# TensorE in the program's own order in one loop, with doubled buffers for attention weights and a longer distance between scores and transposes

## The chip, the cores and the metric

The kernel runs on one core of a Trainium2 chip. Five engines work side by side, each on its own instruction queue: TensorE (PE, matrix products and transposes), VectorE (DVE), ScalarE (ACT), GpSimd (POOL) and SyncE (SP, which here issues all DMA transfers). They tell each other of finished work by semaphores. The metric is the device time of one execution in microseconds (us), median of several.

## The reference

One inference step of a hybrid encoder layer: 2048 prompt frames and 32 sample frames of width 1024, all in 32-bit floats. The input is normalised and modulated, then projected to queries (8 heads of 64), keys and values (2 heads) and an input for a state-space model. One half of the layer is attention in a sliding window, the other half the state-space model with a gate. Both are normalised, joined, and sent through one output projection:

```python
merged = jnp.concatenate([_rmsnorm(attn, lw['attn_out_g']), _rmsnorm(ssm_o, lw['ssm_out_g'])], axis=-1)
x = x + g1 * (merged @ lw['w_out'])
```

with, for the attention,

```python
m = jnp.maximum(jnp.max(s, axis=-1), sink)
p = jnp.exp(s - m[..., None])
p = p / (jnp.sum(p, axis=-1) + jnp.exp(sink - m))[..., None]
o = jnp.einsum('bngrqk,bnkgd->bnqgrd', p, v.astype(jnp.float32))
```

and for the gate `g * sigmoid(g @ ssm_glu_w + ssm_glu_b)` with `g = gelu(ssm_y)`. A feed-forward part (SwiGLU, width 2816) follows and makes up more than half of the time.

## The kernel before

**Precision.** Every product is made of three: each operand is split into a high part that TensorE takes at its fast 32-bit rate (type fp32r) and a low rest, and high x high, high x low and low x high are added up (`mm3`). A split costs one copy, mostly on ScalarE, and one subtraction on VectorE or GpSimd. This is why nearly everything that TensorE makes has to pass through ScalarE and VectorE before TensorE can use it again.

**Stages.** First the input projections with the tables of the state-space model; then the state-space model, 32 groups, with the first six attention tiles beside it; then the loop that the change is about; then the feed-forward part.

**Tiles and flows.** Tokens are worked on in 17 tiles of 128 (the last one is the 32 sample frames), in the order `TILES`: frames 1024 to 2047 first. Each kind of work is written as a Python generator that emits a few instructions and then yields. A `Flow` (L890) holds the generators of one kind that are open: `Flow(make, n, width, lag)` lets at most `width` be open, starts the next one when the youngest has made `lag` steps, and each call of `step` advances every open one by one step, the oldest first.

**One attention tile** (`attention_tile`, L1097). Step 1 loads its rows of queries, keys and values. Step 2 splits and transposes them: the query transposes qb (eight) and the key transposes kb (four). Steps 3 and 4 make the scores s of one half of the queries each (o = 0 and 1), eight matmuls, and call `softmax`: row maxima on VectorE (tile st), exponentials on ScalarE into `pe_[o]` (the trace calls it pbuf), sums and their reciprocal on VectorE, and one multiplication on GpSimd. The next steps, one for each half and each of the two key heads, transpose the weights back through TensorE (`p_split`, L1063: four transposes pt, then the split into th and tl), and after both heads of a half `p_values` multiplies with the values (twelve matmuls ob) and two copies bring the result to the tile att. There are two pbuf buffers, one for each half, and every tile uses the same two. Columns that a half never writes are set to zero once, ahead of all tiles.

**The loop** (the `while True` at L1613) advances four flows in each round, in this order: `fa`, the attention tiles that are still to come; `fp`, the gate of the state-space output (`c_prep`, nine units of 256 frames, so one unit for two tiles; four steps of twelve matmuls cb each, then tanh, products and splits into mh and ml, and a sum of squares ss); `fq`, `c_norm` (sums of squares sa of att, its split into ah and al, and the tiny matmuls rb that turn sums into the factors rso of the two norms); and, in two steps, `fc`, `c_out` (the output projection: two halves of 24 matmuls co for att and 24 for the gate's output, each followed by ScalarE, VectorE and GpSimd and a store). A tile of `c_out` takes five rounds: four with two groups of six co each, and one without. A new attention tile may start only when a tile of `c_out` has ended (six att buffers), so one starts every five rounds. When all attention tiles are done, `h_steps` loads the finished rows xf again and transposes them (ft) for the feed-forward part, at two steps a round.

**Memory of TensorE's results.** Attention takes its result banks in turn from a pair (tag ab) and from the four banks of tag cb, which gate and norms use too; co has two of its own.

**What sets the order.** The generators only set the order in which instructions are emitted. The compiler's planner then makes a plan in time for all engines with its own costs, and each engine's queue is written in the order of that plan, so an instruction emitted later can stand ahead of an earlier one that the plan finds not ready. On the chip each queue then runs strictly in that written order: if an instruction waits, all behind it wait.

Of the kernel before, what the change touches and what calls it, by code (L numbers as in the profile page):

```python
# [10 lines left out]
F32 = mybir.dt.float32  # L11
# [12 lines left out]
NT = NPT + 1  # L24
# [18 lines left out]
NATT = 6  # L43
ASTART = 0
CWS = 2
# [3 lines left out]
CST = 2  # L49
# [8 lines left out]
FA2, CG, WN = 1, 1, 8  # L58
# [15 lines left out]
def hybrid_kernel(  # L74
# [10 lines left out]
    V, A, P, PE, SP = nc.vector, nc.scalar, nc.gpsimd, nc.tensor, nc.sync  # L85
# [17 lines left out]
    def f(a):  # L103
        return a.bitcast(F32)
# [103 lines left out]
    def advance(g, n=1):  # L208
        for _ in range(n):
            if next(g, None) is None:  # L210
                return
# [704 lines left out]
    pb_ = bin_.enter_context(tc.tile_pool(name="pb", bufs=1, reuse_waits="tile", side="right"))  # L916
# [106 lines left out]
    ts(V, nsink, nsink, -1.0)  # L1023
    ts(V, nsinks, nsinks, -1.0)

    pe_ = [pb_.tile([128, 4, 256], F32, name=f"pbuf{o}") for o in range(2)]
    P.memset(pe_[0][:, :, 192:256], 0.0)
    P.memset(pe_[1][:, :, 0:64], 0.0)

    def kv_split(kf, vf, dst, n):  # L1030

# [31 lines left out]
    def p_split(pbuf, kbs, npair, kv):  # L1063

        nc_ = npair * 128
        pt = bbank([128, 2, 256], nm="pt")
        for i in range(npair):
            for kb in kbs:
                PE.transpose(pt[:, kb, i * 128:(i + 1) * 128], pbuf[:, kv * npair + i, kb * 128:kb * 128 + 128], ident)
        th = pb2.tile([128, 2, 256], F32R, tag="th", name="th")  # L1070
        tl = pb2.tile([128, 2, 256], F32R, tag="tl", name="tl")
        k0, k1 = kbs[0], kbs[-1] + 1
        split(th[:, k0:k1, 0:nc_], tl[:, k0:k1, 0:nc_], pt[:, k0:k1, 0:nc_], A, V)
        return th, tl
# [20 lines left out]
    atts = {}  # L1095

    def attention_tile(j):  # L1097
        j = TILES[j]
        n = 128 if j < NPT else DEC
        qkv = pb2.tile([128, QKV], F32, tag="qkv", name="qkv", bufs=1)  # L1100
        SP.dma_start(qkv[0:n], qkv_d[j * 128:j * 128 + n])
        yield 1
        qs = pb2.tile([128, NH, 128], F32R, tag="qs", name="qs", bufs=1)
        qv = qkv[0:n, 0:512].rearrange("p (h d) -> p h d", d=HD)
        split(qs[0:n, :, 0:64], qs[0:n, :, 64:128], qv, A, P)
        qt = pb2.tile([128, NH * 128], F32R, tag="qt", name="qt", bufs=1)
        qw = n // 2 if j < NPT else n
        qtv = qt[:, 0:NH * n].rearrange("p (o h q) -> p h o q", h=NH, q=qw)
        for hb in range(2):
            qb = bbank([128, 4, 128], F32R, nm="qb")  # L1110
            for i in range(4):
                PE.transpose(qb[:, i, 0:n], qs[0:n, hb * 4 + i], identr[0:n, 0:n])
            cp(V if hb else A, qtv[:, hb * 4:hb * 4 + 4], f(qb[:, :, 0:n]).rearrange("p h (o q) -> p h o q", q=qw))
        kf = qkv[0:n, 512:640].rearrange("p (h d) -> p h d", d=HD)
        vf = qkv[0:n, 640:768].rearrange("p (h d) -> p h d", d=HD)
        kt = pb2.tile([128, 4, 256], F32R, tag="kt", name="kt")
        att = pat.tile([128, 4, 128], F32, tag="att", name="att", bufs=NATT)
        atts[j] = att
        if j < NPT:
            vcur = kv_split(kf, vf, kt[:, :, 128:256], n)  # L1120
            if j == TILES[0]:
                pkv = pb2.tile([128, 2, 128], F32, tag="ckv", name="pkv", bufs=1)
                SP.dma_start(pkv, qkv_d[(j - 1) * 128:j * 128, 512:768].rearrange("t (a d) -> t a d", a=2))
                vprev[0] = kv_split(pkv[:, 0].rearrange("p (h d) -> p h d", d=HD),
                                    pkv[:, 1].rearrange("p (h d) -> p h d", d=HD), kt[:, :, 0:128], 128)
            elif j:
                V.tensor_copy(kt[:, :, 0:128], f(vprev[1][:, :, 128:256]))
            vpt = [vprev[0], vcur]
            vprev[0], vprev[1] = vcur, kt
            yield 1  # L1130
            vlist = [(vpt[0], 128), (vcur, 128)]
            kbs = (0, 1) if j else (1,)
            for o in range(2):
                lo, hi = (64 * o, 192 + 64 * o) if j else (128, 192 + 64 * o)
                sp = [bbank([128, 2, 256], nm="s") for _ in range(2)]
                for pr in range(4):
                    for x in range(2):
                        mm(sp[pr // 2][:, pr % 2, lo:hi], qt[:, 512 * o + 128 * pr:512 * o + 128 * pr + 128],
                           kt[:, (pr // 2) * 2 + x, lo:hi], x == 0, x == 1)
                softmax(sp, pe_[o], lo, hi, nsink)  # L1140
                yield 1
            for o in range(2):
                parts = []
                for kv in range(2):
                    parts.append(p_split(pe_[o], kbs, 2, kv))
                    yield 1
                p_values(parts, vlist, kbs, 2, att[:, :, 64 * o:64 * o + 64])
        else:
            ckv = pb2.tile([128, 2, 128], F32, tag="ckv", name="ckv", bufs=1)
            SP.dma_start(ckv[:, 0], cache_k[0, 0].rearrange("t h d -> t (h d)"))  # L1150
            SP.dma_start(ckv[:, 1], cache_v[0, 0].rearrange("t h d -> t (h d)"))
            vc = kv_split(ckv[:, 0].rearrange("p (h d) -> p h d", d=HD), ckv[:, 1].rearrange("p (h d) -> p h d", d=HD),
                          kt[:, :, 0:128], 128)
            vo = kv_split(kf, vf, kt[:, :, 128:160], n)
            sp = bbank([128, 2, 256], nm="s")
            for kv in range(2):
                for x in range(2):
                    mm(sp[:, kv, 0:160], qt[:, 128 * kv:128 * kv + 128], kt[:, kv * 2 + x, 0:160], x == 0, x == 1)
            P.memset(pe_[0][:, 0:2, 160:192], 0.0)
            softmax([sp], pe_[0], 0, 160, nsinks)  # L1160
            yield 1
            parts = [p_split(pe_[0], (0, 1), 1, kv) for kv in range(2)]
            yield 1
            p_values(parts, [(vc, 128), (vo, DEC)], (0, 1), 1, att[:, :, 0:DEC])
        yield 1
# [23 lines left out]
    def stage(nm):  # L1189
        return pw1.tile([128, 512], F32, tag="tc", name=nm, bufs=TC)  # L1190

    fa = Flow(attention_tile, NT, 2, 5)
    n = 0
    while fd.next < fd.n or fd.live:
        for fl, st, lim in ((fm, FM, G), (fd, FDS, G), (fa, FAS, NATT)):
# [21 lines left out]
    cg = chain(glu_steps(wide), wo_steps(range(4), wide, D))  # L1217
# [17 lines left out]
    fp = mbank([128, 64], nm="fp")  # L1235
# [174 lines left out]
    fp_ = {}  # L1410

    def left_open():

        pcg_.close()
        fp_["v"] = ctx.enter_context(tc.tile_pool(name="pfv", bufs=1, reuse_waits="tile", side="right"))

    def ffn_open():

        bin_.close()
        fp_["q"] = ctx.enter_context(tc.tile_pool(name="pfq", bufs=1, reuse_waits="tile", side="right"))  # L1420
        fp_["t"] = ctx.enter_context(tc.tile_pool(name="fst", bufs=2, space=bass.MemoryType.PSUM, reuse_waits="tile"))
# [61 lines left out]
    layers = [Layer(sb, i) for sb in range(3) for i in range(4)]  # L1483
    steps = [(L, u, p) for L in layers for u in range(L.units) for p in range(7)]
    raw, left, right = {}, {}, {}
# [12 lines left out]
    def start_unit(n):  # L1498

        if n < len(steps) and steps[n][0].i == 0:  # L1500
            L, u, _ = steps[n]
            raw[L, u] = [{t: quarter(L, u, m, t, wtile(4)) for t in ("21", "22", "11", "12")} for m in range(2)]
            for r in raw[L, u]:
                r["s1"] = wtile(4)
                tt(P, r["s1"], r["21"], r["22"], ADD)
                tt(P, r["21"], r["11"], r["21"], SUB)
                r["s3"] = r["21"]
# [99 lines left out]
    cg = wo_steps(range(4, 8), stage, 512)  # L1607
    fp = Flow(c_prep, 9, 1, 0)
    fq = Flow(c_norm, NT, 1, 0)
    fc = Flow(c_out, NT, 1, 0)  # L1610
    wn = 0
    hg = [None]
    while True:  # L1613
        more = fa.step(fc.done() + NATT)
        fp.step(fc.done() // 2 + 2)
        for _ in range(CWS):
            wn += 1
            advance(cg)
        fq.step(min(fa.done(), 2 * fp.done(), fc.done() + 2))
        if wn > WN:  # L1620
            for _ in range(CST):
                more = fc.step(fq.done()) or more
        if fa.next == fa.n and not fa.live:
            if hg[0] is None:
                ffn_open()
                hg[0] = h_steps(0)
            elif fc.done() >= 6:
                if (layers[0], 0) not in raw:
                    start_unit(0)
                advance(hg[0], 2)  # L1630
                if fp.next == fp.n and not fp.live and "v" not in fp_:
                    left_open()
                    prepare(0)
        if not more:
            break
    if hg[0] is None:
        ffn_open()
        hg[0] = h_steps(0)
# [199 lines left out]
```

## Time and profile before

| | us |
|---|---|
| median of 3 runs | 2383.77 (2382.73 to 2385.17) |
| profiled execution | 2380.64, its span 2378.8 |
| TensorE busy | 2221.1 (93%) |
| VectorE busy | 1802.9 (76%) |
| ScalarE busy | 1259.6 (53%) |
| GpSimd busy | 1349.8 (57%) |
| first co | 572.45 |
| last att of the loop | 894 |
| first matmul of the feed-forward part | 963 |

Busy shares are averages over stages with different limits; a matmul's time in the trace also contains its way through the array, so the distance from start to start tells more of the rate than a matmul's own duration. The trace's columns in the lists by time are: start, length, engine, line, operation, what is written and read, shapes, count, and in brackets the idle time of the engine before it and what ended it.

### The profile page before, as it was taken

Reading aid. Unit: us, or ns where it says so; the run is one execution under the profiler, and the core shown is the slowest. Engines: PE = TensorE matmul, PEld = TensorE weight load, DVE = VectorE, ACT = ScalarE, POOL = GpSimd, SP = SyncE. Lnnn points to the kernel's source line nnn. Section 1 sums busy time; section 2 is a strip of 40 time slices with the busy share of each in tenths; the row PEclk is TensorE's granted clock in tenths of the full one; section 3 lists DMA queues with packets and bytes.
Section 4 is the critical chain, followed back from the end, with each engine's and each line's share of the span. In section 5 each row is a group of like instructions: output and inputs, shape, how many; then the busy total and the mean of one; then the engine's idle time right before and its main releaser. Section 6 shows DMA issues by size and latency. Waiting matters only on the chain. (4 is left out here: it accounts for less than half of the span.)

```text
span 2378.8 us, 39058 instructions
## 1 busy us (share of the span) xinstructions
PE 2221.1 (93%) x13262; PEld 2058.2 (87%) x13262; DVE 1802.9 (76%) x2722; ACT 1259.6 (53%) x2549; POOL 1349.8 (57%) x1205
## 2 busy tenths in 40 slices
PE   7898998997999999699999998999999989999998
PEld 4577777786888878598999998999999979999998
DVE  6878876777777765877768879666688896777887
ACT  5655534556556556433445556444455754444663
POOL 1277765785655656899654236655532375665232
PEclk8898998999899999799999999999999999999999
DMA  7757767875312214698335644543355435434653
GB/s 229 264 169 232 205 202 220 250 229 157 91 56 76 78 49 153 198 277 252 116 108 159 195 141 151 172 139 101 112 184 174 132 122 175 134 95 121 193 158 123
DMA packets 429572, 380.12 MB, mean 160 GB/s; under 512 B 57326, under 2 KB 358986, under 8 KB 429372
## 3 DMA queue, kind: packets, MB, share of 16 engines
q1 hardware_dynamic: 429372, 377.63, 51.9%
q8 instruction: 104, 1.70, 0.3%
q14 instruction: 96, 0.79, 0.1%
HBM read 284.63 MB, written 92.91 MB: 159 GB/s over the span
## 5 line engine op out<-in xcount | busy, mean ns | idle before, releaser
L89 DVE TENSOR_TENSOR wl<-wr,wh 128x512 fp32r<-128x512 f32 (+1 forms) x714 | 736.0, 1048 | 220.4 <-ACT wh L101 217.5
L101 ACT ACTIVATE wh<-wr 128x512 fp32r<-128x512 f32 (+1 forms) x714 | 434.6, 616 | 540.6 <-PE fx L117 303.2
L117 PE MATMUL fx<-bh,wh 128*128 128x352 f32 (+1 forms) x1584 | 511.6, 323 | 9.7 <-ACT c L101 5.8
L117 PE MATMUL fx<-bl,wh 128*128 128x352 f32 (+1 forms) x1584 | 509.5, 322 | 3.5 <-DVE bl L89 3.5
L117 PE MATMUL fx<-bh,wl 128*128 128x352 f32 (+1 forms) x1584 | 510.3, 322 | 0.0
L89 POOL TENSOR_TENSOR wr<-wr 128x512 f32<-128x512 f32 x264 | 392.6, 1495 | 165.7 <-DVE wl L89 148.0
L117 PEld LDWEIGHTS fx<-bh,wh 128*128 128x128 f32 x1584 | 300.3, 190 | 11.7 <-ACT c L101 6.5
L117 PEld LDWEIGHTS fx<-bl,wh 128*128 128x128 f32 x1584 | 300.0, 189 | 4.1 <-DVE bl L89 4.0
L117 PEld LDWEIGHTS fx<-bh,wl 128*128 128x128 f32 x1584 | 299.5, 189 | 0.1
L117 PE MATMUL fy<-bh,wh 128*128 128x352 f32 (+1 forms) x792 | 255.6, 323 | 2.9 <-DVE acc L98 2.6
L117 PE MATMUL fy<-bh,wl 128*128 128x352 f32 (+1 forms) x792 | 255.0, 322 | 0.1
L117 PE MATMUL fy<-bl,wh 128*128 128x352 f32 (+1 forms) x792 | 254.8, 322 | 0.0
L89 POOL TENSOR_TENSOR c<-c 128x352 f32<-128x352 f32 (+1 forms) x99 | 146.7, 1482 | 173.1 <-ACT wh L101 107.9
L89 POOL TENSOR_TENSOR c<-c,acc 128x352 f32<-128x352 f32 (+1 forms) x72 | 84.5, 1178 | 173.3 <-ACT c L101 169.8
L89 POOL TENSOR_TENSOR q<-q,q 128x1408 f32<-128x1408 f32 (+3 forms) x24 | 86.2, 3596 | 122.9 <-DVE q L89 86.8
L117 PEld LDWEIGHTS fy<-bh,wh 128*128 128x128 f32 x792 | 150.2, 190 | 3.4 <-DVE acc L98 2.9
L89 DVE TENSOR_TENSOR bl<-q,bh 128x1408 fp32r<-128x1408 f32 (+3 forms) x84 | 149.4, 1780 | 5.0 <-ACT bh L101 5.0
L117 PEld LDWEIGHTS fy<-bl,wh 128*128 128x128 f32 x792 | 150.0, 189 | 0.0
L117 PEld LDWEIGHTS fy<-bh,wl 128*128 128x128 f32 x792 | 149.5, 189 | 0.5 <-DVE wl L89 0.4
L117 PE MATMUL fz<-bh,wl 128*128 128x352 f32 (+1 forms) x396 | 130.5, 330 | 10.9 <-DVE wl L89 10.7
L117 PE MATMUL fz<-bh,wh 128*128 128x352 f32 (+1 forms) x396 | 129.5, 328 | 6.5 <-ACT wh L101 6.5
L101 ACT ACTIVATE bh<-q 128x1408 fp32r<-128x1408 f32 (+3 forms) x84 | 107.6, 1284 | 50.3 <-DVE q L89 29.1
(384 smaller groups left out, 5236.3 us busy)
## 6 DMA issues: line engine op xcount, KB each, us to landing
wr<-in_w_gate_dram SPq DMA_DIRECT2D x132, 256.0 KB
wr<-in_w_up_dram SPq DMA_DIRECT2D x132, 256.0 KB
wr<-sd_d SPq DMA_DIRECT2D x96, 256.0 KB
wr<-in_w_down_dram SPq DMA_DIRECT2D x72, 256.0 KB
adw<-in_w_ada_dram SPq DMA_DIRECT2D x64, 256.0 KB
f_d<-c SPq DMA_DIRECT2D x88, 176.0 KB
sm<-sm_d SPq DMA_DIRECT2D x32, 448.0 KB
q<-f_d SPq DMA_DIRECT2D x16, 704.0 KB
```

The costliest lines, as they stand in the source:

```text
L89: e.tensor_tensor(out, a, b, op=op)
L101: A.activation(out, a, func, **kw)
L117: PE.matmul(out, lhsT, rhs, start=start, stop=stop, skip_group_check=more)
```

## The change

It has three parts. The pair of pbuf buffers exists twice, and even and odd tiles take turns. The attention flow may hold three open tiles instead of two, and a tile has two more steps that emit nothing: one between its scores and the first transposes of its weights, one between the last such transposes and the last product with the values. And the whole loop stands in a region in which TensorE's instructions keep the order in which the program emits them; the order of the other engines, and how TensorE's instructions from outside the region fall among them, stay the planner's.

```diff
-    pe_ = [pb_.tile([128, 4, 256], F32, name=f"pbuf{o}") for o in range(2)]
-    P.memset(pe_[0][:, :, 192:256], 0.0)
-    P.memset(pe_[1][:, :, 0:64], 0.0)
+    pes = [[pb_.tile([128, 4, 256], F32, name=f"pbuf{i}{o}") for o in range(2)] for i in range(2)]
+    for pe_ in pes:
+        P.memset(pe_[0][:, :, 192:256], 0.0)
+        P.memset(pe_[1][:, :, 0:64], 0.0)
...
     def attention_tile(j):
+        pe_ = pes[j % 2]
         j = TILES[j]
...
                 softmax(sp, pe_[o], lo, hi, nsink)
                 yield 1
+            yield 1
             for o in range(2):
                 parts = []
                 for kv in range(2):
                     parts.append(p_split(pe_[o], kbs, 2, kv))
+                    yield 1
+                if o:
                     yield 1
                 p_values(parts, vlist, kbs, 2, att[:, :, 64 * o:64 * o + 64])
...
-    fa = Flow(attention_tile, NT, 2, 5)
+    fa = Flow(attention_tile, NT, 3, 5)
...
-    while True:
-        more = fa.step(fc.done() + NATT)
...
+    with tc.manual_schedule(engines={PE.engine}):
+        while True:
+            more = fa.step(fc.done() + NATT)
...
```

The body of the loop is the same but for its indent.

More of the change, by code (lines that the diff above doesn't have):

```diff
@@ L1612, in hybrid_kernel @@
     hg = [None]
-    while True:
-        more = fa.step(fc.done() + NATT)
[L1615 to L1635, printed above, removed]
+    with tc.manual_schedule(engines={PE.engine}):
+        while True:
+            more = fa.step(fc.done() + NATT)
+            fp.step(fc.done() // 2 + 2)
+            for _ in range(CWS):
+                wn += 1
+                advance(cg)
+            fq.step(min(fa.done(), 2 * fp.done(), fc.done() + 2))
+            if wn > WN:
+                for _ in range(CST):
+                    more = fc.step(fq.done()) or more
+            if fa.next == fa.n and not fa.live:
+                if hg[0] is None:
+                    ffn_open()
+                    hg[0] = h_steps(0)
+                elif fc.done() >= 6:
+                    if (layers[0], 0) not in raw:
+                        start_unit(0)
+                    advance(hg[0], 2)
+                    if fp.next == fp.n and not fp.live and "v" not in fp_:
+                        left_open()
+                        prepare(0)
+            if not more:
+                break
     if hg[0] is None:
```

## The prediction

> **What bounds the kernel now.** I read the page first, then the busy time by stretches, then TensorE's waits in the one stretch that the change touches, then the instructions around those waits in order of time.
>
> ```profile
> span 2378.8 us, 39058 instructions
> 640.00:890.00 250.00, 229.35 (x1432) 203.78 (x1432) 182.49 (x312) 136.76 (x397) 148.39 (x133) 0.95 0.20 64
> 888.10:963.00 74.90, 70.80 (x390) 57.87 (x391) 38.82 (x56) 42.75 (x83) 51.65 (x47) 0.96 0.48 158
> ```
>
> The loop of attention, gate and output projection runs from about 565 to 963 us. In its steady part (640 to 890) the columns after the length are the busy times of TensorE, its weight loads, VectorE, ScalarE and GpSimd, then the granted clock. TensorE is busy 229 of 250 us, VectorE only 182: TensorE sets the length, so what can be won there is its idle time, 20.7 us, and what the clock of 0.95 costs, 250 x 0.05 = 12.5 us. The tail (888 to 963) is as tight, and the feed-forward part follows it. I take that part to move as a block with the loop's end.
>
> ```profile
> PE pt L1069 <- POOL pbuf L89: 10.8, 4, 5.3
> PE pt L1069 <- DVE st L89: 3.7, 1, 3.7
> PE co L117 <- DVE t L98: 2.2, 2, 1.1
> PE ob L117 <- DVE tl L89: 2.0, 1, 2.0
> ```
>
> These are TensorE's waits of 640 to 890: 18.7 us, and 14.5 of it before pt, the transposes of the attention weights, which wait for the normalised weights pbuf. Two such places, with the last gate matmul (cb) ahead of each:
>
> ```profile
> 675.33 0.28 PE L117 MATMUL cb<-gh,gll 128*128 128x256 f32 x1
> ...
> 682.02 0.97 PE L117 MATMUL s<-kt,qt 128*128 128x64 f32 x8
> ...
> 686.91 0.39 PE L117 MATMUL ob<-tl,vs 128*128 128x256 f32 x1 [2.04 <-DVE tl L89]
> ...
> 688.88 0.63 PE L117 MATMUL co<-woh,ml 128*128 128x512 f32 x1
> ...
> 693.18 0.69 PE L1069 MATMUL pt<-cpk,pbuf 128*128 128x128 f32 x2 [3.67 <-DVE st L89]
> ...
> 720.04 0.28 PE L117 MATMUL cb<-gl,glh 128*128 128x256 f32 x1
> ...
> 721.22 0.28 PE L117 MATMUL cb<-gh,gll 128*128 128x256 f32 x1
> ...
> 722.52 0.46 PE L1112 MATMUL qb<-identr,qs 128*128 128x128 f32 x4
> ...
> 723.53 0.47 PE L117 MATMUL co<-wol,ah 128*128 128x512 f32 x1
> ...
> 727.50 1.03 PE L117 MATMUL s<-kt,qt 128*128 128x192 f32 x8
> ...
> 730.92 0.42 PE L117 MATMUL co<-woh,ah 128*128 128x512 f32 x1
> ...
> 736.19 0.39 PE L117 MATMUL co<-woh,ml 128*128 128x512 f32 x1
> 741.85 1.12 PE L1069 MATMUL pt<-cpk,pbuf 128*128 128x128 f32 x4 [5.27 <-POOL pbuf L89]
> ```
>
> I number attention tiles from 0 in the order worked on; these are 8 and 10. From the first score matmul (s) to the first pt it takes 693.18 - 682.02 = 11.2 us and 741.85 - 727.50 = 14.35 us. It is the even tiles that stall, because a gate unit serves two tiles and its end throws a burst of splits at VectorE, ahead of the row maxima that the softmax needs:
>
> ```profile
> 735.23 1.64 DVE L89 TENSOR_TENSOR gl<-gr,gh 128x512 fp32r<-128x512 f32 x1
> ...
> 737.36 0.16 DVE L89 TENSOR_TENSOR st<-st,nsink 128x4 f32<-128x4 f32 x1
> ```
>
> The minimum that starts tile 10's softmax (st) comes ten us after its scores. Tiles 12 and 14 do the same, odd tile 9 does not:
>
> ```profile
> 703.08 1.03 PE L117 MATMUL s<-kt,qt 128*128 128x192 f32 x8
> ...
> 775.77 1.48 PE L117 MATMUL s<-kt,qt 128*128 128x192 f32 x12
> ...
> 790.49 0.77 PE L1069 MATMUL pt<-cpk,pbuf 128*128 128x128 f32 x5 [0.18 <-POOL pbuf L89]
> ...
> 826.64 1.03 PE L117 MATMUL s<-kt,qt 128*128 128x192 f32 x8
> ...
> 840.37 0.90 PE L1069 MATMUL pt<-cpk,pbuf 128*128 128x128 f32 x3 [4.87 <-POOL pbuf L89]
> ```
> ```profile
> 710.17 1.47 POOL L89 TENSOR_TENSOR pbuf<-pbuf,st 128x768 f32<-128x768 f32 x1
> ```
>
> That is 14.7 and 13.7 us for 12 and 14, and 710.17 + 1.47 - 703.08 = 8.55 us for 9.
>
> **The change part by part.** *Doubled buffers and a third live tile.* Two more memsets on GpSimd:
>
> ```profile
> L1027 POOL MEMSET pbuf<- 128x256 f32 x1 | 0.3, 317 | 5.6 <-PE adv L117 5.6
> ```
>
> Two at 0.32 us, behind 5.6 us of idle time: nothing, 0.6 us without that cover. A buffer alone also wins nothing here, since exp does not wait for pt to free pbuf:
>
> ```profile
> L101 ACT ACTIVATE pbuf<-s,st 128x192 f32<-128x192 f32 (+3 forms) x77 | 30.7, 412 | 33.8 <-DVE st L89 31.7 <-PE cb L117 2.1
> ```
>
> 31.7 of the 33.8 us are VectorE's minima. The buffers only make the longer distance legal. Tiles still start every five rounds of the loop, so each round's work stays the same. No DMA and no arithmetic is added, and the queues of SP and the other engines stay the planner's.
>
> *TensorE in program order, distance one round longer.* I laid out the rounds from the code, with prices from the rows: co (736.19 - 730.92)/23 = 0.229 us, so the 12 of a round 2.75; cb (721.22 - 720.04)/10 = 0.118, so 12 of them, or the 12 ob of equal width, 1.42; four each of qb, kb and pt take 723.53 - 722.52 = 1.01, so a qb/kb set of 12 is 1.0 and a pt group 0.34; eight s at most 1.0. For an even tile the order between the last cb and its s is: co, pt, qb/kb, co, ob, pt = 2.75 + 0.34 + 1.0 + 2.75 + 1.42 + 0.34 = 8.6 us. Now it is 682.02 - 675.45 = 6.6 and 727.50 - 721.34 = 6.2 us. So the scores come 2.0 to 2.4 us later behind the burst (2.2 for tiles 12 and 14), and I take as much off their latency. Between s and pt lie s, co, pt, s, co, rb (0.34), ob = 1.0 + 2.75 + 0.34 + 1.0 + 2.75 + 0.34 + 1.42 = 9.6 us, where tile 8 has now about 5.5 of work and tile 10 has 9.1. What is left to wait: tile 8: 11.2 - 2.0 - 9.6 < 0, none; tile 10: 14.35 - 2.4 - 9.6 = 2.35; tile 12: 14.7 - 2.2 - 9.6 = 2.9; tile 14: 13.7 - 2.2 - 9.6 = 1.9. Tile 6 is the first started in the loop and has no other tile around it, only s, co, s, co = 7.5 us:
>
> ```profile
> 641.60 2.89 POOL L89 TENSOR_TENSOR pbuf<-pbuf,st 128x768 f32<-128x768 f32 x2
> ```
> ```profile
> 631.39 1.03 PE L117 MATMUL s<-kt,qt 128*128 128x192 f32 x8
> ...
> 645.90 1.36 PE L1069 MATMUL pt<-cpk,pbuf 128*128 128x128 f32 x11
> ```
>
> Its weights come after 641.60 + 1.45 - 631.39 = 11.7 us, a wait of 4.2; but nobody wanted them before 645.90, and with tile 9's 8.55 it would be 1.05. I take the middle, 2.6. Sum 9.75, against 18.7 now: **-8.95 us**. Bounds: -18.7 if VectorE keeps pace, +1 if the latencies do not shrink with the later scores (1.6 + 4.75 + 5.1 + 4.1 + 4.2 = 19.8).
>
> *Clock.* co takes 0.63 us at 688.88, after a gap, against 0.39 at 736.19. I give back the clock loss in the share of the waits that goes, 8.95/18.7 = 0.48 of 12.5: **-6.0 us** (bounds 0 and -12.5). The Trainium skill ("TensorE: Matmul & The Clock Gate", HAM oscillation) would have only idle gaps above about 3.4 us cost clock. By it, of the five waits that I leave (2.6 us the middle one for tile 6) none would, and this term would be -12.5. The trace speaks against it: the slow co at 688.88 follows a gap of 2.04 us, not yet the one of 3.67.
>
> *Start of the loop.* The planner now pulls output matmuls ahead of the small matmul rb of the first tile. Program order puts rb of a tile before its first co:
>
> ```profile
> 572.45 0.50 PE L117 MATMUL co<-woh,ah 128*128 128x512 f32 x1
> ...
> 601.27 0.63 PE L117 MATMUL co<-woh,mh 128*128 128x512 f32 x1
> ...
> 603.92 0.42 PE L117 MATMUL rb<-cols,sa 128*128 128x2 f32 x2
> ```
>
> 19 co run there before rb, 19 x 0.229 = 4.35 us, which will stand behind it. In return 12 cb of the next gate unit come ahead, 1.4 us: **+2.9 us** (bounds 0, if VectorE gets to rb's sums earlier; 6 at the half clock of these gaps). Queued behind rb is then all of co; the tiles still open from before the loop can fill.
>
> *Tail.* The transposes ft that prepare the feed-forward part (six loads in two groups of three, three buffers) also come in program order:
>
> ```profile
> 924.38 0.55 PE L1446 MATMUL ft<-cpk,xf 128*128 128x128 f32 x3
> ```
> ```profile
> 931.78 1.15 ACT L101 ACTIVATE xf<-xf,r 128x1024 f32<-128x1024 f32 x1 [0.50 <-DMA xf<-x_d]
> ```
>
> From the first group's last ft to the second's last scaled row: 931.78 + 1.15 - 924.93 = 8.0 us. Program order leaves one round of co and rb between, 3.1 us; TensorE waits 4.9, with co behind it, where now the planner runs co and cb: **+4.9 us** (bounds 0 and 8).
>
> *Before the loop* (tiles 0 to 5 beside the state-space work) the planner keeps its freedom. I know no sign: 0, some us either way.
>
> Sum: -8.95 - 6.0 + 2.9 + 4.9 = -7.15 on the profiled execution's 2380.64 (span 2378.8 and 1.84 around it), 2373.5. That execution lies 3.13 below the median of 2383.77, so **2376.6 us** on the median's scale, 0.30% faster. Own range 2366 to 2383.
>
> **The rivals.**
>
> *The backlog wins (slower).* Place: pt of the even tiles. If VectorE's burst goes with the scores, latencies stay at 11 to 14.7 us and all waits remain at 19.8: +1.1, no clock back, and start and tail pay in full: +1.1 + 2.9 + 4.9 = +8.9, 2392.7. It decides once the mean latency of tiles 8 to 14 stays above about 12.5 us. For it: VectorE is already busy 182 of 250 us and TensorE can no longer run anything else ahead of a waiting pt. Against it: the odd tiles' 8.55 us. More bank waits of the same kind would carry it to 2398.
>
> *All waits go.* -18.7 - 12.5 + 2.9 + 4.9 = -23.4: 2360.4. It needs VectorE to finish 182 us of work in about 219, 83%. The Trainium skill ("Perfetto Trace Analysis", Optimization Strategy) reads a gap that keeps repeating as possibly a buffer too few, and two buffers would then end it as here. The ScalarE row above, with VectorE as releaser and not pt, speaks against it.
>
> *It does not act.* The new order is nearly the planner's, or new gaps are as large as the old: 2383.8.
>
> **How the numbers follow.** Forecast 0.45, backlog 0.25, all waits go 0.18, no action 0.12. A median here tells 0.2%, 4.8 us, from no change. Of the forecast's own spread 0.7 lies beyond that, 0.22 within, 0.08 slower: faster 0.45 x 0.7 + 0.18 = 0.50; within 0.10 + 0.10 = 0.20; slower 0.04 + 0.25 + 0.01 = 0.30. The range, 2355 to 2398, reaches past the second and third case.
>
> **What would show it.** Right: in the changed trace the five waits of pt for pbuf fall below 10 us together, the clock of the steady part rises to 0.97 or more, co starts only after the first rb, and one wait of ft for xf of some 5 us appears. The forecast is wrong if pt still waits 4 us or more at each even tile, if ob waits for tl in most tiles (the row of 686.91 as a habit), or if s waits for kt; and its tail term is wrong if ft never waits.

## The result and the profile after

The changed kernel takes 2407.54 us (median of 4 runs, 2402.01 to 2409.55), the kernel before, in runs beside it, 2383.25 us (2381.97 to 2385.17). The ratio is 1.0099, with an interval of 1.0081 to 1.0116: 1% slower. The forecast was 2376.6 with a range up to 2398, so it was wrong in sign and size. The profiled execution took 2402.01, the lowest of the four, so the two traces show 21.4 of the 24.3 us between the medians. One execution of e9_alloc further down (2463.01 us, at a granted clock of 0.83) was slow, and the median given there is that of its nine others.

To see where the 21.4 us between the two spans arise, I cut both traces at four events: the last gelu of the state-space part (t<-y), the first rb, the last att, and the first matmul of the feed-forward part (fx). The rows are busy times by stretches; behind start, end and length come TensorE, its weight loads, VectorE, ScalarE and GpSimd, then the granted clock, the DMA share and GB/s. Before the change:

```profile
355.00:558.80 203.80, 182.88 (x1130) 157.81 (x1128) 143.44 (x316) 104.73 (x249) 148.73 (x270) 0.94 0.71 216
558.80:603.90 45.10, 31.40 (x161) 24.46 (x162) 38.64 (x62) 32.17 (x74) 16.60 (x12) 0.79 0.59 186
603.90:894.20 290.30, 268.91 (x1666) 238.94 (x1665) 213.75 (x357) 156.91 (x442) 171.91 (x154) 0.94 0.23 70
894.20:963.00 68.80, 64.99 (x349) 52.59 (x348) 35.85 (x51) 40.65 (x78) 48.92 (x43) 0.96 0.47 154
```

After it, with the span:

```profile
core 0 of [0], span 2400.2 us
355.00:579.10 224.10, 189.10 (x1128) 163.72 (x1127) 155.09 (x333) 120.44 (x276) 153.98 (x273) 0.90 0.69 214
579.10:620.40 41.30, 29.50 (x156) 25.71 (x155) 32.19 (x52) 25.98 (x58) 12.68 (x11) 0.71 0.38 105
620.40:902.80 282.40, 263.52 (x1623) 232.25 (x1622) 194.03 (x346) 153.20 (x433) 162.54 (x149) 0.95 0.23 71
902.80:983.80 81.00, 74.08 (x393) 60.59 (x392) 32.92 (x52) 41.49 (x80) 49.58 (x47) 0.96 0.39 131
```

The state-space part with the first six attention tiles is 20.3 us longer. The start of the loop is 3.8 shorter, the middle 7.9 shorter, the tail 12.2 longer, and the feed-forward part behind it moves as a block (2378.8 - 963.0 = 1415.8, now 2400.2 - 983.8 = 1416.4). So in these traces nearly the whole loss already stands at the last gelu, and the loop itself wins nothing; the experiments show that a late gelu alone would not have cost this. The matmul counts show why the shorter middle is no gain: it has 43 fewer, and the tail has 44 more. Of co alone, the output projection, the tail now holds 23 more; before and after:

```profile
894.20:963.00 68.80, 52.03 (x200) 0.96 0.47 154
```
```profile
902.80:983.80 81.00, 56.38 (x223) 0.96 0.39 131
```

The 19 co that used to run ahead of the first rb are held behind it. They are not what makes the tail longer: in e7_middle below, 24 co run ahead of the first rb, and the tail has 223 all the same. A stretch that depends less on these shifts is the steady part of 640 to 890 us, the one that the prediction argued from. First its busy times after the change, then TensorE's waits in it:

```profile
640.00:890.00 250.00, 231.51 (x1437) 203.94 (x1436) 180.52 (x324) 142.57 (x410) 151.19 (x138) 0.95 0.23 70
```
```profile
PE pt L1070 <- POOL pbuf L89: 5.2, 1, 5.2
PE ob L117 <- DVE tl L89: 3.9, 6, 1.5
PE ob L117 <- ACT th L101: 3.0, 3, 1.5
PE kb L1039 <- DVE ks L89: 2.8, 1, 2.8
PE kb L1039 <- ACT ks L101: 1.8, 1, 1.8
PE rb L117 <- ACT pbuf L101: 0.8, 1, 0.8
```

TensorE is busy 231.51 us where it was 229.35, at the same granted clock of 0.95. The waits of pt fell from 14.5 us to 5.2 as intended, but ob (the products with the values) now waits 6.9 us for the split weights th and tl, all of it at the odd tiles 7, 9, 11 and 13, kb 4.6 us for the split keys, and the sum hardly moves: all rows of this view, the small ones too, give 18.3 us where they gave 21.3 (the prediction quoted the four largest, 18.7). How one wait became another is seen around the even tiles 10, 12 and 14 (list by time; brackets: idle time before, and its releaser):

```profile
746.71 0.38 PE L117 MATMUL rb<-cols,sa 128*128 128x2 f32 x2 [0.82 <-ACT pbuf L101]
...
749.19 0.80 PE L117 MATMUL ob<-th,vs 128*128 128x256 f32 x2 [1.05 <-ACT th L101]
751.07 0.58 PE L117 MATMUL ob<-tl,vs 128*128 128x256 f32 x1 [1.09 <-DVE tl L89]
...
752.09 1.05 PE L1070 MATMUL pt<-cpk,pbuf 128*128 128x128 f32 x4
...
798.84 0.51 PE L117 MATMUL ob<-th,vs 128*128 128x256 f32 x2 [0.47 <-ACT th L101]
799.56 0.39 PE L117 MATMUL ob<-tl,vs 128*128 128x256 f32 x1 [0.22 <-DVE tl L89]
...
800.20 0.66 PE L1070 MATMUL pt<-cpk,pbuf 128*128 128x128 f32 x4
...
845.62 0.50 PE L117 MATMUL ob<-th,vs 128*128 128x256 f32 x2 [1.50 <-ACT th L101]
846.34 0.39 PE L117 MATMUL ob<-tl,vs 128*128 128x256 f32 x1 [0.22 <-DVE tl L89]
...
847.05 0.66 PE L1070 MATMUL pt<-cpk,pbuf 128*128 128x128 f32 x4
```

At these tiles pt has no bracket any more. But the products of the tile before stand right ahead of it, and they wait 2.96 us with rb at tile 10, 0.7 at tile 12, 1.7 at tile 14. I read this as ScalarE and VectorE being late with everything in these moments: whichever instruction comes first in the fixed order takes the wait. This is argued from the rows; no run tests it alone.

### The profile page after: what moved, and what is told of

Its sections match the earlier page's. It is cut to its first block, busy times and chain, and to the rows that moved or that the text cites. A ratio compares the mean times of both kernels' runs of the same rounds, so it can differ in the third digit from the quotient of the medians.

```text
span 2400.2 us, 39064 instructions
## 1 busy us (share of the span) xinstructions
PE 2227.0 (93%) x13262; PEld 2064.4 (86%) x13262; DVE 1778.3 (74%) x2722; ACT 1266.5 (53%) x2555; POOL 1347.0 (56%) x1207
## 5 line engine op out<-in xcount | busy, mean ns | idle before, releaser
L117 PE MATMUL fz<-bh,wl 128*128 128x352 f32 (+1 forms) x396 | 130.8, 331 | 10.5 <-DVE wl L89 10.4
```

What stands on the lines that cost most here:

```text
L117: PE.matmul(out, lhsT, rhs, start=start, stop=stop, skip_group_check=more)
```

## The experiments

Three theories stood at the beginning. A: the longer tiles cost time before the loop, where they mix with the state-space groups. B: the second pair of buffers (8 KB) delays the first loads. C: TensorE in program order costs time in the loop. Medians of the kernel before in the four groups of runs were 2380.51, 2381.89, 2382.44 and 2382.99 us; each ratio is against its own group.

**The three parts alone.** One kernel has the region only; one has everything but the region; one has only the second pair, with the flow as before.

```diff
 # e1_region: the kernel before
-    while True:
+    with tc.manual_schedule(engines={PE.engine}):
+        while True:
 # e2_noregion: the changed kernel
-    with tc.manual_schedule(engines={PE.engine}):
+    if True:
 # e3_buffers: the kernel before
+    pes = [[pb_.tile([128, 4, 256], F32, name=f"pbuf{i}{o}") for o in range(2)] for i in range(2)]
+        pe_ = pes[j % 2]
```

> The kernel before with the TensorE region alone: one pair of pbuf, two open tiles, short distance. Theory A (the longer tiles cost before the loop, where they mix with the state-space groups): the loop starts as before (last gelu near 559 us), total 2380 to 2392. Theory B (the 8 KB of the second pair of buffers shifts memory and delays the first loads): total 2380 to 2392 too. Theory C (TensorE in program order costs): 2400 or more, with the extra time behind 560 us.

> The changed kernel without the region: doubled pbuf, three open tiles, two empty steps, TensorE left to the planner. Theory A: last gelu near 579 us and 2400 to 2408, as with the whole change. Theory B: the same. Theory C: 2380 to 2388.

> The kernel before with the second pair of pbuf alone, even and odd tiles in turn. Theory A: 2380 to 2388, first query load near 358 us. Theory B: first query load near 370 us and 2395 or more. Theory C: 2380 to 2388.

Measured: region alone 2394.77 us (ratio 1.0054, 1.0036 to 1.0073), no region 2366.60 (0.9934, 0.9913 to 0.9956), second pair alone 2369.48 (0.9943, 0.9923 to 0.9963). C has the direction right but not the numbers: the region costs 14 us on the kernel before, and 41 within the changed kernel, yet 2394.77 lies between C's range and that of A and B, and the other two kernels are faster than any theory had them. B falls: the second pair makes the kernel faster. A fares oddly: without the region the last gelu is also late (583.3 us), and yet that kernel is fast. The late state-space part is a loss only together with the region.

**The long distance only in the loop.** The empty steps from tile 6 on, and the third open tile from the beginning of the loop; the region as in the changed kernel.

```diff
+        far = j >= NATT
-            yield 1
+            if far:
+                yield 1
-                if o:
+                if o and far:
-    fa = Flow(attention_tile, NT, 3, 5)
+    fa = Flow(attention_tile, NT, 2, 5)
...
+    fa.width = 3
```

> The whole change, but the two empty steps and the third open tile only for the tiles that start in the loop (number 6 on); the first six as before. Theory A: last gelu near 559 us, total 2378 to 2390. Theory B: 2395 or more, the first query load stays near 370 us. Theory C: 2400 or more.

2390.45 us (1.0033, 1.0018 to 1.0048), at the end of A's range: 17.1 us of the loss go when the six tiles ahead of the loop are short. The rows by stretches from the last gelu on, cut at the same events:

```profile
563.20:606.80 43.60, 26.23 (x134) 23.49 (x133) 35.95 (x63) 31.51 (x71) 10.36 (x10) 0.66 0.54 158
606.80:890.20 283.40, 267.04 (x1655) 235.69 (x1656) 196.34 (x354) 156.89 (x443) 164.01 (x151) 0.96 0.24 71
890.20:971.20 81.00, 74.17 (x393) 60.49 (x393) 32.66 (x52) 41.50 (x80) 49.62 (x47) 0.96 0.39 131
```

The first rb comes 13.6 us earlier than in the changed kernel (606.8 against 620.4), and what follows has the same length: 2388.4 - 606.8 = 1781.6 us to the end, against 1779.8.

**The same without the region, and its two halves.** Here the planner orders TensorE everywhere; then the empty steps for all tiles, and the third open tile from the start, each alone.

```diff
 # e5_late_noregion: e4_late
-    with tc.manual_schedule(engines={PE.engine}):
+    if True:
 # e6_steps: e5_late_noregion
-        far = j >= NATT
+        far = True
 # e8_width: e5_late_noregion
-    fa = Flow(attention_tile, NT, 2, 5)
+    fa = Flow(attention_tile, NT, 3, 5)
```

> Buffers, empty steps and third open tile, but the steps and the third tile only for tiles 6 to 16 (those of the loop), and no region: the planner orders TensorE everywhere. Theory A2 (the losses add up from two places: what the longer distance costs the six tiles beside the state-space groups, and what the region costs in the loop): the last gelu comes at about 561 to 565 us as in the runs with short early tiles, and the loop takes the 365 us that it took with the long distance and the planner's order, so the span is 563 + 365 + 1416 = 2344, time about 2346. Rival (the short loop of the run without the region was short only because the loop's tiles had been worked ahead during its longer time before the loop): the loop gives back what the first part wins, and the time stays at 2362 to 2368.

> As the run before it, but the two empty steps are there for all tiles; the third open tile still only from the loop on. It tells which of the two parts delays the state-space groups. If the empty steps do (a tile's scores, weights and products fall in other rounds than the groups' own exponentials), the last gelu comes at about 580 us and the time is about 2363. If the third open tile does, the last gelu stays at 561 to 565 us and the time at about 2346.

> The other half of the pair: three open tiles from the start, the empty steps only for the tiles of the loop. If the third open tile delays the state-space groups, the last gelu comes at about 580 us and the time is about 2363; if the empty steps do, the last gelu stays at 561 to 565 us and the time at about 2346. If both stay early, it is the two together.

2364.40 us (0.9922, 0.9907 to 0.9937), 2365.89 (0.9938, 0.9919 to 0.9958) and 2364.11 (0.9919, 0.9902 to 0.9936). The sum that I had made from two kernels, 2346, failed: the rival was right, and without the region it doesn't matter whether the early tiles are long. The last gelu comes at 561.4, 570.0 and 563.2 us and the last att at 881.3, 880.4 and 884.3, so the loop takes back what was lost ahead of it. How far it can is seen in e2_noregion, which differs from the changed kernel by the region alone and has long early tiles; from its first rb to its last att:

```profile
617.70:883.20 265.50, 261.91 (x1686) 232.36 (x1685) 202.76 (x356) 157.58 (x445) 173.23 (x157) 1.00 0.25 74
```

TensorE is idle for 3.6 us there, at a clock of 1.00, where the changed kernel has 18.9 us at 0.95 and 63 matmuls fewer in 16.9 us more. What lets the planner fill this loop so well, no run shows.

The third open tile alone does nothing: the order of TensorE, ScalarE and VectorE in the third kernel is instruction for instruction that of the first. These kernels, with the one without the region above, are the fastest of the study, 0.8% faster than before. The stretches of e5_late_noregion from the first rb on:

```profile
599.50:881.30 281.80, 270.93 (x1691) 239.47 (x1690) 212.60 (x362) 158.76 (x455) 174.06 (x157) 0.97 0.25 75
881.30:945.20 63.90, 61.71 (x336) 49.84 (x334) 35.08 (x47) 35.22 (x70) 41.78 (x38) 0.97 0.43 144
```

Against the kernel with the region the middle is as long, but holds 36 matmuls more, and the tail is 17 us shorter.

**The region in parts.** First only from the end of the first output tile to the end of attention; then also at the start (without the first of the three calls below); the whole loop is e4_late.

```diff
+    def loop(until):
+        nonlocal wn
+        while not until():
...
+    loop(lambda: fc.done() >= 1)
+    with tc.manual_schedule(engines={PE.engine}):
+        loop(lambda: fa.next == fa.n and not fa.live)
+    loop(lambda: False)
```

> Short early tiles, long distance in the loop, and the region only around the middle of the loop: it begins when the first tile of the output projection has ended and ends when the last attention tile has ended; start and tail are the planner's. With the region around the whole loop this kernel took 408 us from the last gelu to the first feed-forward matmul (time 2390); without any region 365 are expected. If the region costs at start and tail, as predicted (there by the output products held behind the first rb, and by ft), this run takes about 365 to 372 us there and 2346 to 2353 in all. If it costs in the steady part, by waits that the planner would have filled, the middle stays as long as with the whole region: about 385 to 395 us and 2366 to 2376.

> Short early tiles, long distance, and the region from the beginning of the loop up to the end of the last attention tile; the tail is the planner's. With the region to the very end: 2390.5; with it in the middle alone: 2375.6; without it: 2364.4. If the tail's order (ft ahead of output products, one wait for xf after the other) is what costs at the end, this run wins the 5 to 10 us of the tail: 2378 to 2385, and ft waits less than 1 us. If the long tail is work that the middle has left over (33 co and 18 cb more behind the last att), the work behind the last att stays at some 65 us and the run wins only what ft waits, about 5 us: 2384 to 2387. The start then keeps its share of 5 us against the region in the middle alone.

2375.59 us (0.9968, 0.9949 to 0.9987) and 2381.25 (1.0001, 0.9985 to 1.0017). With 2364.40 without a region and 2390.45 with the whole one, the region costs by medians 11.2 us in the middle, 5.7 at the start, 9.2 in the tail; the intervals of the two runs here just overlap, so the 5.7 is the least sure. The traces agree that it is all three places. Up to the last gelu the order is the same in all these kernels; from there to the end they take 1799.3 and 1801.4 us without a region (e5_late_noregion and e8_width, which have one order), 1808.5 with it in the middle, 1814.2 with the start, 1825.2 with the tail (1827.7 in e15_rwidth, which has the same order): about 8, 6 and 11 or more.

The first run fell in the range of a loss in the steady part, but that range took 365 us for the loop without a region, and it is 383.8 and 385.0. From the last gelu to the first fx e7_middle takes 387.6, only some 3 us more. The rest of its loss stands in the feed-forward part (1420.9 us against 1415.5 and 1416.4), where two kernels of one order, e3_buffers and e9_alloc, differ by 3.5; so how much of it is the region's is not shown. The second run fell in the range of a loss by the tail's order. The tail of e12_head by stretches:

```profile
883.10:953.70 70.60, 70.26 (x392) 57.88 (x392) 33.30 (x48) 40.19 (x78) 48.26 (x44) 1.00 0.44 145
```

and the wait of ft in its tail, then in that of e4_late:

```profile
PE ft L1453 <- ACT xf L101: 0.3, 1, 0.3
```
```profile
PE ft L1453 <- ACT xf L101: 6.8, 5, 1.9
```

Freed, the tail runs 392 matmuls (e4_late: 393) in 70.6 us instead of 81.0: ft no longer waits 6.8 us, and the clock stays at 1.00. But it still has 392 and not 336, since the middle has held back output products: of co alone the tail has 222 or 223 in e4_late, e7_middle and e12_head, and 188 in e5_late_noregion. I read the region's cost in the middle so: where an instruction would wait, the planner's order has co in front of it, and the program's order has not. At the start, the 24 co that e7_middle runs ahead of the first rb run in the middle of e12_head (579 co there against 556); that middle is 4.2 us longer, and the way from the last gelu to the first rb 2.6.

**One more round between transposes and products.** It asks whether ob's new waits are only a distance too short.

```diff
 # e10_ob: e4_late
-                if o and far:
-                    yield 1
+                if far:
+                    yield 1
+                    if o:
+                        yield 1
```

> The changed kernel with short early tiles (2390 us) and one more empty step in each tile of the loop ahead of both products with the values (so one round between the last transposes and the products of the first half is two, of the second half three). In the loop under program order TensorE waited 4.2 us for tl, 3.1 for th (ob), 2.3 for pbuf (pt). Theory D (these waits are there because the distance is a round too short): the waits of ob fall below 2 us and the time to 2383 to 2386. Rival V (the splits come late in the bursts of ScalarE and VectorE, whatever the distance, or other operands - kb, rb - are late in their place): idle time of TensorE from the first rb to the last att stays at 14 to 18 us, and the time at 2388 to 2394.

2387.90 us (1.0030, 1.0012 to 1.0047), 2.5 less than e4_late, with intervals that overlap. The waits between the first rb and the last att:

```profile
PE rb L117 <- DVE sa L1363: 3.3, 1, 3.3
PE kb L1039 <- DVE ks L89: 3.3, 1, 3.3
PE pt L1070 <- POOL pbuf L89: 2.8, 2, 2.3
PE ob L117 <- DVE tl L89: 2.8, 3, 1.1
PE kb L1039 <- ACT ks L101: 1.3, 1, 1.3
PE pt L1070 <- ACT pbuf L101: 1.1, 1, 1.1
```

The waits of ob fall from 7.6 us to 2.8, so distance does cure part of them, but pt, kb and rb keep theirs (11.8 us, 11.6 in e4_late). TensorE is idle for 284.3 - 271.8 = 12.5 us of this stretch (16.4 in e4_late), less than the rival allowed, and the time lies between the two ranges. Neither theory came out cleanly: the distance cures what it is put in front of, and no more.

**The second pair, not used, and the memsets alone.**

```diff
 # e9_alloc: e3_buffers
-        pe_ = pes[j % 2]
+        pe_ = pes[0]
 # e13_memset: the kernel before
+    for _ in range(2):
         P.memset(pe_[0][:, :, 192:256], 0.0)
         P.memset(pe_[1][:, :, 0:64], 0.0)
```

> The kernel before with the second pair of pbuf buffers allocated and zeroed, but every tile goes on using the first pair. It tells what the gain of the doubled buffers by themselves (2369.5, a ratio of 0.9943) comes from. Theory F (freedom: with a second pair the plan may put a tile's exponentials ahead of the last transposes of the tile before): without the use of the pair the gain goes, 2378 to 2385. Rival P (another plan: the shifted addresses and two more memsets alone lead to another order and to a later first load, whatever the pair is used for): 2366 to 2374.

> The kernel before with each of its two pbuf memsets issued twice, and no second pair. The second pair, allocated and zeroed but not used, gave 2369.7 us, and its tiles' first transposes came at 378.5 us instead of 367.3. Theory S (space: the 8 KB move the other buffers of that side, and another order follows): without the allocation the time is that of before, 2378 to 2385, and the first qb at 367 us. Rival M (two more instructions are enough to tip the plan): 2365 to 2374.

2369.03 us (0.9938, 0.9916 to 0.9961) and 2381.28 (0.9986, 0.9971 to 1.0001). A pair that nobody uses gives the whole gain of the pair that is used, and the two kernels run the same order on TensorE, ScalarE and VectorE. Two more memsets give nothing, with the order of before. So the gain of 11 to 13 us comes with the allocation and not with its use: the plan comes out otherwise, from the first attention tile on. That this is because other buffers move, as Theory S has it, is argued; the traces hold no addresses. In the steady part (640 to 890) the waits of pt for pbuf are 7.3 us with the pair in use and 7.9 with it unused, where the kernel before has 14.5 for pt. The first transposes, before and with the unused pair:

```profile
367.33 0.89 PE L1112 MATMUL qb<-identr,qs 128*128 128x128 f32 x8
```
```profile
378.47 0.79 PE L1114 MATMUL qb<-identr,qs 128*128 128x128 f32 x8
```

The first tile starts 11 us later, about as B had it, and the kernel is faster all the same. Which of the many differences of that plan wins isn't settled.

**What is late ahead of the loop.** The changed kernel with short tiles 0 and 1 only; then the empty steps for all tiles, and the third tile from the start, each alone beside the region.

```diff
 # e11_first2: e4_late with Flow(attention_tile, NT, 3, 5)
-        far = j >= NATT
+        far = j >= 2
 # e14_rsteps: e4_late
-        far = j >= NATT
+        far = True
 # e15_rwidth: e4_late
-    fa = Flow(attention_tile, NT, 2, 5)
+    fa = Flow(attention_tile, NT, 3, 5)
```

> The changed kernel, with the two empty steps left out for the first two attention tiles only; tiles 2 to 5 beside the state-space groups have them, and the third open tile is allowed from the start. In the changed kernel the last gelu comes 20 us late, and ScalarE stands still for 7.4 us at 424 to 431 us, ahead of the exponentials of the second tile, with gelus queued behind. Theory O (that one stall at the first two tiles is the cause): the last gelu comes at 561 to 568 us and the time is 2388 to 2396, as with all six short. Rival E (each long tile among the groups costs some us): the last gelu comes at 572 to 580 us and the time is 2400 to 2408.

> The changed kernel with a third open tile only from the loop on; the empty steps for all tiles. In the changed kernel the first rb comes at 620.4 us, with short early tiles at 606.8, and from it to the end both take 1780 to 1782 us. If the empty steps make it late: first rb at 617 to 622, time 2402 to 2408. If the third open tile does: first rb at 605 to 609, time 2388 to 2392.

> The other half: three open tiles from the start, empty steps only for the tiles of the loop. If the third open tile makes the first rb late: 617 to 622 us, time 2402 to 2408. If the empty steps do: first rb at 605 to 609 us, time 2388 to 2392. If the first rb is early in both halves, only the two together cost.

2400.63 us (1.0080, 1.0053 to 1.0106), 2399.04 (1.0069, 1.0049 to 1.0089) and 2390.45 (1.0033, 1.0021 to 1.0044). The stall that I suspected is this one of the changed kernel (ScalarE, by time; the load of the table of functions for the exponentials waits in the queue, and the gelus behind it):

```profile
431.17 1.28 ACT L101 ACT_TABLE_LOAD   x1 [7.42 <-DVE st L89]
...
434.69 0.39 ACT L101 ACTIVATE t<-y 128x262 f32<-128x262 f32 x1
```

It isn't the cause of the loss. With two short tiles the last gelu is back at 561.7 us, and still the first rb comes late and the time is 2400.63. The stretch between the two:

```profile
561.70:616.20 54.50, 30.51 (x171) 26.81 (x170) 44.72 (x75) 35.79 (x85) 16.85 (x13) 0.67 0.53 168
```

Here the attention work is what comes late: 171 matmuls instead of 134 are left for the start of the loop, where TensorE is busy 30.5 of 54.5 us. (With empty steps for all, it is 131, and there the last gelu is late, at 574.7.) So the mark that goes best with the time is the first rb, not the last gelu: 606.8 us in e4_late, 610.2 with empty steps for all, 616.2 here, 620.4 in the changed kernel, and the rest takes 1780 to 1787 us in all four. It is a rough mark: e15_rwidth and e12_head have e4_late's order up to there and come to it at 604.7 and 600.8, and of the 7.4 us between the spans of e14_rsteps and e4_late only 3.4 lie ahead of it. The third open tile by itself changes nothing (the order is that of e4_late, and so is the median, 2390.45); the empty steps cost 8.6 us, less than was expected of them alone, with the first rb between the two ranges, and a third open tile on top of them another 8.5.

## Why the prediction was wrong

The medians make a ladder from the kernel before to the changed one: second pair allocated -11 to -13, each against its own group (2369.5 and 2369.0), empty steps and third tile in the loop under the planner -5 (2364.4, intervals that overlap), region in the middle +11.2, at the start +5.7, in the tail +9.2 (2390.45), empty steps for the first six tiles +8.6 (2399.04), the third tile for these +8.5 (2407.54). The steps add up to the whole by construction, their sizes depend on the order in which they are taken, and each is good to a few us. Against it the prediction's terms:

- **Before the loop: 0 in the prediction, +17.1 measured.** This is the largest step that failed. "The planner keeps its freedom" is right for the order, but two empty steps more make every early tile longer by two rounds, and under the region nothing makes up for a late first rb. The prediction gave "some us either way" and no bound from a row. The region has its share in it: without it the same long early tiles cost 2.2 us (2366.60 against 2364.40), and it costs 26.0 us with short early tiles and 40.9 with long ones. So some 15 us arise from the two together and from neither alone, and the prediction had no term for that.
- **Steady part: -8.95 and -6.0; measured some 2 us, and none in the clock.** The waits of pt behaved as worked out, better even: 5.2 us remain, all at tile 6, where I had 2.6 and at most 4.2; at tiles 10, 12 and 14 I left 2.35, 2.9 and 1.9, and there is none. But I counted only the waits that the row of before named. In the new order the instruction ahead of pt waits instead: 2.96, 0.7 and 1.7 us, 5.4 together where I had 7.15 for pt; and kb and ob add 4.6 us and more elsewhere. Of the 8.95, moreover, 4.2 were the waits of co and ob, which the sum let end without a row for it; those of co did end, and those of ob rose from 2.3 us to 7.3. So idle time fell by 2 to 3 us only, and the clock stayed (0.95, where 0.97 was the sign of a right forecast). The prediction had named "ob waits for tl in most tiles" as what would make it wrong; ob waited for tl 6 times and for th 3 times, at every odd tile from 7 to 13 and at no even one.
- **The comparison behind that term.** With the same buffers and distance the region around the middle alone costs 11.2 us against the planner's order (2375.59 and 2364.40). I priced the region against the old order, and not against the planner's order for the new flow.
- **Start: +2.9 predicted, +5.7 measured**, within its bounds of 0 to 6, as far as the two medians are told apart. The held co were seen rightly (the first co now starts at 623.2, behind the first rb at 620.4), and so was their price, about their own run time: e12_head shows 4.2 us for them in the middle and 2.6 ahead of the first rb. The planner's order for the new flow has 24 of them there, not 19.
- **Tail: +4.9 predicted, +9.2 measured**, above its bound of 8, and 10.4 between the two traces (81.0 and 70.6 us). The mechanism is the predicted one, ft waiting for xf with co behind it; in the changed kernel it is five waits of 6.9 us in all instead of one of 4.9, and the clock falls to 0.96 with them.
- **Doubled buffers alone: 0 predicted, -11 to -13 measured.** The reasoning on the buffer's use was right, since a pair in use and a pair not in use give the same order and, within their intervals, the same time. What it left out is that an allocation alone can turn the plan.

The rivals: "the backlog wins" had the sign and the place next door, but it wanted pt itself to go on waiting, and its 2392.7 had no part before the loop. The Trainium skill's remark that a repeating gap can mean too few buffers ("Perfetto Trace Analysis", Optimization Strategy), which stood beside "all waits go", isn't borne out here: the waits of pt for pbuf fall to 7.3 us with another pair in use and to 7.9 with the same pair not in use.

## What to carry to other kernels

Here, fixing an engine's order didn't remove the waits that I put down to other engines' backlog; they moved to the instruction ahead in line, and the filler that the planner would have put there was gone. Compare such a region with what the planner does under the same new freedom, not with the old kernel. And before a gain of half a percent is put down to a new buffer, allocate it and leave it unused: here that control gave the whole gain. And a loss can belong to two changes together: take them out one by one in both orders before one of them is blamed.

## What was not expected of the hardware

The cost of a gap in TensorE's clock is not set by the length of the gap alone. Two kernels, e5_late_noregion and e6_steps, come to the same instructions with the same gap near the end of attention. The rows by stretches of 4 us are TensorE's busy time, its count, the granted clock, DMA share and GB/s. The first kernel's wait, and the stretches behind it:

```profile
863.84 1.97 PE L1070 MATMUL pt<-cpk,pbuf 128*128 128x128 f32 x8 [3.29 <-POOL pbuf L89]
```
```profile
864.00:868.00 4.00, 4.00 (x20) 0.50 0.02 9
...
876.00:880.00 4.00, 4.00 (x11) 0.50 0.98 287
880.00:884.00 4.00, 4.00 (x26) 0.94 1.19 305
```

The second kernel's:

```profile
868.46 1.89 PE L1070 MATMUL pt<-cpk,pbuf 128*128 128x128 f32 x8 [3.32 <-POOL pbuf L89]
```
```profile
868.00:872.00 4.00, 3.54 (x17) 0.57 0.16 57
872.00:876.00 4.00, 4.00 (x32) 1.00 0.01 2
```

After 3.29 us the clock stays at half for some 16.5 us, though TensorE is busy without a break; after 3.32 us it is back within 3.5. It isn't the chance of one execution: e8_width, with the first kernel's order, has a gap of 3.30 us there, and a clock of 0.50 from 868 to 880 us. The Trainium skill ("TensorE: Matmul & The Clock Gate", What's actually happening) has a free-running window of about 3.4 us, half speed for what is issued in the first such stretch of work, and full speed for everything after. The second kernel agrees with that, the first does not: it was busy for almost five such windows at half clock. One such case costs about 8 us, an estimate (half of 16.5), so a part of the differences of a few us between kernels may be of this kind; what makes the first case longer stays open.

How far medians scatter shows in four pairs of kernels with the same order on TensorE, ScalarE and VectorE: 2369.48 and 2369.03, 2364.40 and 2364.11, 2390.45 and 2390.45, and 2382.99 and 2381.28 us (the kernel before and e13_memset); the kernel before alone has four medians 2.5 us apart. Single executions scatter more: the nine of e9_alloc lie between 2362.08 and 2379.49 us.
